# A last mixture-of-experts expert that norms its own rows, on one Trainium2 core

## The chip, the core and the metric

The kernel runs on one core of a Trainium2 chip. The metric is the device time of one execution in microseconds (us), over several runs. The engines are TensorE (PE, with its weight loads shown as PEld), VectorE (DVE), ScalarE (ACT), GpSimd (POOL) and SyncE (SP). DMAs are issued by SP, ACT and POOL; an issue takes its place in its engine's order, so an engine that waits before an issue does nothing else meanwhile.

## The reference

One post-norm layer over 512 tokens of 1024 features in float32: a layer norm, three mixers (differential attention, gated delta rule, S5), an output projection, a layer norm, and then a mixture of experts, whose sum is added to its own input and normed again:

```python
for e in range(16):
    hid = silu(h @ w1[e]) * (h @ w3[e])
    ffn += comb[:, e:e+1] * (hid @ w2[e])      # comb: 2 experts of 16 a token, else 0
out = layer_norm(ALPHA * h + ffn, ln2_g, ln2_b)
```

The change lies in the last two lines: when the sum of a token's row is complete, and when it is normed and stored. The kernel works on the row divided by ALPHA, which the norm's epsilon allows for.

## The kernel before, in words

Everything is in `tile_layer`. Up to some 495 us of the trace it computes the mixers, the first norm and the routing; the routing sorts the tokens into slots of each expert. `hdr` and `yd` (in DRAM) both hold the normed rows: `hdr` is what the experts read, `yd` is the running sum of row and experts.

**The experts.** Sixteen experts run one after the other. A "large" one has 128 slots and splits its weights into a high and a low part (`split`, ACT `e_hi` and DVE `e_lo`), a "small" one has 64 slots and uses them as loaded. Of the last three, 13 is large, 14 and 15 are small. `gather` (L1494) fetches an expert's token rows by an indirect DMA of POOL, and `turn_x` transposes them (ACT `xth`). Each expert has 12 weight chunks of 512 KB: 0 to 7 ("up": w1 and w3), after which ACT makes the Silu (`hid`) and DVE the product; `turn_h` transposes it (`hhh`); 8 to 11 ("down": w2) give its output in PSUM (`pS`). `finish` and `finish2` scale that by the token's weight (ACT, `y`, one buffer) and `scatter` (L1499) adds it to rows of `yd` by an indirect DMA of POOL that accumulates; a small expert's slots hold half rows, 64 on the first half of the partitions and 64 on the second.

**The order.** `steps` (L1606 to 1611) lists the 192 chunks: ups of expert e, then downs of e-1. The loads go out in that order on SP (`ahead`, L1632) into a ring of 34 buffers, whose places are given by `RING` (L42). The buffers are memory of the stage before, so the first load into each waits until that stage has done with it; load 28 also waits for the first two gathers (`FIRST`, L55). N is 192.

**The end.** Experts 0 to 13 are scattered, 14 and 15 are not: `y_parts` (L1697) splits their scaled output into a high and a low part, and one-hot matrices (built at step N-20 by POOL's iota and DVE) put their rows by matmuls onto PSUM banks (`add_y`, L1741), on top of the rows of `yd`, which SP loads as soon as scatter 13 has landed (L1734). The norm's parameters are loaded by SP after them (L1737). The four tiles of 128 rows are then normed from PSUM, spread over DVE, ACT and POOL (`sum_v`, `square_a`, `centre`, `rsqrt_a`, `last`), and SP stores them in seven pieces (`put`, L1845).

Of the kernel before, what the change touches and what calls it, by code (L numbers as in the profile page):

```python
# [21 lines left out]
P = 128  # L22
D = 1024
S = 512
# [17 lines left out]
RING = (2, 8, 15, 14, 21, 13, 12, 11, 9, 10, 29, 3, 7, 30, 18, 31, 16, 17, 19, 20, 27, 28, 6, 32, 33, 0, 1, 4, 5, 22, 23, 24, 25, 26)  # L42
OHT = 20
HT = 9
# [35 lines left out]
def tile_layer(ctx: ExitStack, tc: tile.TileContext, a, out):  # L80
# [157 lines left out]

    def place_init(e):
        e.memset(sb16[:, 0:64], 0.0)  # L240
        e.memset(half2[0:SL], 8192.0)
        e.memset(half2[SL:P], 8193.0)
        e.memset(fold2, 0.0)
        for h in range(2):
            e.tensor_copy(fold2[0:SL, h * SL:(h + 1) * SL], ident[0:SL, 0:SL])

# [1336 lines left out]
    def turn2(x, own=False):  # L1583
# [3 lines left out]
        h = halves(traw())[0] if own else exs("hhh", F32)  # L1587
        act(h[:, 0:4 * SL], p[:, 0:4 * SL], AF.Copy)
        return h
# [10 lines left out]
    def turn_h(e):  # L1600
        hts[e] = turn2(hid[e], e == NE - 1) if small[e] else turn(hid[e], "hh")
# [46 lines left out]
    def step(i):  # L1648
# [3 lines left out]
        if c < 8:  # L1652
# [11 lines left out]
            if c == 7:  # L1664
# [8 lines left out]
                if e == 0:  # L1673
                    turn_h(e)
        else:
# [6 lines left out]
            if e == NE - 2 and c == HT:  # L1682
                turn_h(e + 1)
            if c == 11:
                if e + 1 < NE - 1:
                    turn_h(e + 1)
                if e < NE - 2:
                    (finish2 if small[e] else finish)(pys[e][0] if small[e] else pys[e], at(1, e), at(0, e))
                else:
                    y_parts(e)  # L1690


    li = [ex.tile([P, 1], F32, name="li%d" % i) for i in range(2)]
    oht = []
    yps = {}

    def y_parts(e):  # L1697

        comb, p = at(1, e), pys[e][0]
        yh, yl = yps[e] = halves(traw(F32R))  # L1700
        act(yh, p, AF.Copy, scale=comb)
        stt(yl, p, comb, f32(yh), ALU.mult, ALU.subtract)
        tt(xgs[e % 2][:, 0:512], f32(yh), f32(yl), ALU.add, e=gp)

    with tc.manual_schedule():
# [7 lines left out]
        for i in range(N - 4):  # L1713
# [4 lines left out]
            if i == N - OHT:  # L1718
                io = traw()[:, 0:S]
                gp.iota(io, pattern=[[1, S]], base=-4096, channel_multiplier=0, allow_small_or_imprecise_dtypes=True)  # L1720
                oht.extend(halves(traw(F32R)))
                for j in range(2):

                    nc.vector.tensor_copy(li[j], at(0, NE - 2 + j))
                    ts(li[j], li[j], half2, ALU.subtract, 0.5, ALU.mult)
                    ts(oht[j], io, li[j], ALU.is_equal)
                nc.vector.tensor_copy(cnti, most)


    with tc.manual_schedule():  # L1730
        xs = {}
        for t in TORD:
            xs[t] = traw()
            nc.sync.dma_start(xs[t], yd[t * P:(t + 1) * P, :])  # L1734
        g2 = [traw(), traw()]
        for x, y in zip(g2, ("ln2_g", "ln2_b")):
            nc.sync.dma_start(x, a[y].partition_broadcast(P))  # L1737
        junk = [traw() for _ in range(2)]
        zs = {}

        def add_y(t, e):  # L1741

            for i, y in enumerate(yps[e]):
                for n in range(2):
                    r = slice(n * SL, (n + 1) * SL)
                    mm(zs[t][n], oht[e - NE + 2][r, t * P:(t + 1) * P], y[r], e < NE - 1 and i == 0, e == NE - 1 and i == 1)

        def pre(t):
            zs[t] = [psT(), psT()] if t == 3 else psS() if t == 1 else psA((NE - 1 + t // 2) % 2)
            add_y(t, NE - 2)  # L1750

        def add_h(t):

            for n in range(2):
                mm(zs[t][n], ident, xs[t][:, n * 512:n * 512 + 512], False, False)

        for i in range(N - 4, N):
            ahead(i + 1, CASTS2)
            step(i)
        act(junk[0][:, 0:1], pcol, AF.Copy)  # L1760
        table()

        for t in TORD[0:3]:
            pre(t)
        add_y(TORD[0], NE - 1)
        add_y(TORD[1], NE - 1)
        add_h(TORD[2])
        add_y(TORD[2], NE - 1)
        pre(TORD[3])
        add_h(TORD[3])  # L1770
        add_y(TORD[3], NE - 1)

        def exv(name, n):
            return ex.tile([P, n], F32, name=name)


        var, rr = {}, {}

        def pair(x):
            v, r = exv("var%d" % x, 2), exv("rr%d" % x, 2)  # L1780
            for j, t in enumerate((x, x + 1)):
                var[t], rr[t] = v[:, j:j + 1], r[:, j:j + 1]
            return v, r

        P0, P1 = pair(0), pair(2)

        def rsqrt_a(v, x):

            w, y, q = exv("w%d" % x, 2), exv("y%d" % x, 2), exv("q%d" % x, 2)
            ts(w, v, 1.0, ALU.mult, EPS2, ALU.add)  # L1790
            act(y, w, AF.Ln)
            act(y, y, AF.Exp, scale=-0.5)

            def end(r):
                tt(q, y, y, ALU.mult)
                tt(q, q, w, ALU.mult)
                ts(q, q, -0.5, ALU.mult, 1.5, ALU.add)
                tt(r, q, y, ALU.mult)

            return end  # L1800

        EPS2 = LN_EPS / ALPHA ** 2
        st = {t: ex.tile([P, 2, 6], F32, name="st%d" % t) for t in (2,)}
        mv = {t: exv("mv%d" % t, 2) for t in (2,)}
        hs, hq, nm = ({t: exv("%s%d" % (n, t), 2) for t in (0, 1, 3)} for n in ("hs", "hq", "nm"))

        def half(c):
            return slice(c * 512, c * 512 + 512)

        def bn(t, c):  # L1810
            nc.vector.bn_stats(st[t][:, c, :], zs[t][c])  # L1811

        def bn_end(t):
            nc.vector.bn_aggr(mv[t], st[t].rearrange("p a b -> p (a b)"))  # L1814
            nc.vector.tensor_copy(var[t], mv[t][:, 1:2])  # L1815

        def sum_v(t):

            for c in range(2):
                x = xs[t][:, half(c)]  # L1820
                nc.vector.scalar_tensor_tensor(x, zs[t][c], 1.0, x, ALU.mult, ALU.add, accum_out=hs[t][:, c:c + 1])
            zs[t] = halves(xs[t])

        def sum_a(t):
            for c in range(2):
                act(junk[0][:, half(c)], zs[t][c], AF.Identity, accum_out=hs[t][:, c:c + 1])

        def sum_end(t):

            ts(nm[t][:, 0:1], hs[t][:, 0:1], hs[t][:, 1:2], ALU.add, -1.0 / (32 * D), ALU.mult)  # L1830
            ts(nm[t][:, 1:2], hs[t][:, 0:1], hs[t][:, 1:2], ALU.add, -1.0 / D, ALU.mult)

        def square_a(t):

            for c in range(2):
                act(junk[0][:, half(c)], zs[t][c], AF.Square, scale=1.0 / 32, bias=nm[t][:, 0:1],
                    accum_out=hq[t][:, c:c + 1])

        def square_end(t):
            tt(var[t], hq[t][:, 0:1], hq[t][:, 1:2], ALU.add)  # L1840

        def centre(t, m, op, c):
            stt(xs[t][:, half(c)], zs[t][c], m, g2[0][:, half(c)], op, ALU.mult)

        def put(t, c):  # L1845
            nc.sync.dma_start(out[0, t * P:(t + 1) * P, c], xs[t][:, c])

        def last(t):
            for c in range(2):
                x = xs[t][:, half(c)]  # L1850
                stt(x, x, rr[t], g2[1][:, half(c)], ALU.mult, ALU.add)
                put(t, half(c))

        sum_v(1)
        sum_end(1)
        square_a(1)
        sum_v(0)
        xs[0] = junk[1]
        sum_end(0)
        square_a(0)  # L1860
        for c in range(2):
            centre(0, nm[0][:, 1:2], ALU.add, c)
        square_end(1)
        square_end(0)
        end = rsqrt_a(P0[0], 0)
        sum_a(3)
        end(P0[1])
        nb = exv("nb", 1)
        tt(nb, nm[1][:, 1:2], rr[1], ALU.mult)
        for c in range(2):  # L1870
            act(xs[1][:, half(c)], zs[1][c], AF.Identity, scale=rr[1], bias=nb)
        last(0)
        sum_end(3)
        for c in range(2):
            centre(3, nm[3][:, 1:2], ALU.add, c)
        square_a(3)
        for x, op in ((0, ALU.mult), (1, ALU.add)):
            for c in range(2):
                x_ = xs[1][:, half(c)]
                tt(x_, x_, g2[x][:, half(c)], op, e=gp)  # L1880
# [130 lines left out]
```

## Time and profile before

| | us |
|---|---|
| median of 3 runs | 772.11 (771.17 to 775.31) |
| the profiled execution | 778.69 |
| its span in the trace | 777.0 |
| PE busy / DVE / ACT / POOL, of the span | 685.4 / 523.8 / 352.9 / 101.6 |

The profiled execution is 1.7 us longer than its span, and 6.6 us over the median; all times in the rows are from the start of the span. Busy shares are means over stages with different limits. The experts' stage is 495 to 762 us, and what the change touches is from there to the end.

### The profile page before, as it was taken

How to read it: one execution, taken by the hardware profiler on the slowest of the kernel's cores; microseconds unless marked ns; L12 is line 12 of the kernel's file. 1: busy time of each engine (PE TensorE's matmuls, PEld its weight loads, DVE VectorE, ACT ScalarE, POOL GpSimd, SP SyncE). 2: the span in 40 equal slices, each digit the busy share in tenths (PEclk: the TensorE clock that was granted, in tenths of full speed). 3: DMA queues.
4: the chain of work that ended last, by engine and by line, in shares of the span. 5: the costliest groups of instructions: out<-in, count | busy, mean ns of one | idle time of the engine just before them, and what ended most of it. 6: DMA issues, size and time to landing. Idle time of an engine off the chain costs nothing. (4 is left out here: it accounts for less than half of the span.)

```text
span 777.0 us, 10787 instructions
## 1 busy us (share of the span) xinstructions
PE 685.4 (88%) x3560; PEld 499.1 (64%) x3560; DVE 523.8 (67%) x1375; ACT 352.9 (45%) x572; POOL 101.6 (13%) x138
## 2 busy tenths in 40 slices
PE   0999949999899799999899975789999999999881
PEld 0667737786788576667687754668655767677420
DVE  6899997786753445566737888879454577677326
ACT  2579632723111522155523321568464577566323
POOL 6010000000000011111000012111131132112112
PEclk9999978997778999959779995699999999999996
DMA  6142304120101257517314239899999999999983
GB/s 218 47 141 73 118 1 124 34 65 28 55 1 51 73 154 184 177 37 198 131 42 178 94 134 417 324 411 326 351 394 385 386 383 356 393 349 387 385 312 114
DMA packets 54271, 155.98 MB, mean 201 GB/s; under 512 B 13528, under 2 KB 13784, under 8 KB 54208
## 3 DMA queue, kind: packets, MB, share of 16 engines
q1 hardware_dynamic: 38960, 124.26, 42.1%
q0 software_dynamic: 8192, 19.08, 9.3%
q10 hardware_dynamic: 7056, 11.88, 5.1%
q8 instruction: 30, 0.49, 0.2%
q14 instruction: 33, 0.27, 0.1%
HBM read 139.98 MB, written 19.14 MB: 205 GB/s over the span
## 5 line engine op out<-in xcount | busy, mean ns | idle before, releaser
L84 DVE TENSOR_TENSOR e_lo<-e_raw,e_hi 128x1024 fp32r<-128x1024 f32 x108 | 128.7, 1222 | 28.3 <-ACT e_hi L95 24.6
L95 ACT ACTIVATE e_hi<-e_raw 128x1024 fp32r<-128x1024 f32 x108 | 111.7, 1061 | 29.0 <-PE pA L101 9.1
L101 PE MATMUL pA<-hTh,w_lo 128*128 128x512 f32 x184 | 76.8, 419 | 12.3 <-DVE w_lo L84 12.3
L101 PE MATMUL pA<-hTh,w_hi 128*128 128x512 f32 x184 | 78.3, 426 | 2.5 <-DVE cv L92 1.1
L101 PE MATMUL pA<-hTl,w_hi 128*128 128x512 f32 x184 | 75.5, 411 | 0.0
L101 PE MATMUL pA<-e_hi,xth 128*128 128x512 f32 x144 | 58.2, 404 | 0.0
L101 PE MATMUL pA<-e_lo,xth 128*128 128x512 f32 x144 | 57.1, 397 | 0.1
L101 PE MATMUL pA<-e_hi,xtl 128*128 128x512 f32 x144 | 57.2, 397 | 0.0
L101 PE MATMUL pA<-e_raw,xth 128*64 128x512 f32 x224 | 50.4, 596 | 0.0
L101 PEld LDWEIGHTS pA<-hTh,w_lo 128*128 128x128 f32 x184 | 36.3, 197 | 20.5 <-DVE w_lo L84 12.9
L95 ACT ACTIVATE w_hi<-w_raw 128x1024 fp32r<-128x1024 f32 x29 | 30.6, 1054 | 34.9 <-PE pA L101 26.0
L1500 POOL DMA_INDIRECT yd__140<-y,tab x14 | 23.2, 1658 | 172.0 <-ACT y L95 159.1
L101 PEld LDWEIGHTS pA<-hTh,w_hi 128*128 128x128 f32 x184 | 36.3, 197 | 12.6 <-issue 2.3
L101 PEld LDWEIGHTS pA<-hTl,w_hi 128*128 128x128 f32 x184 | 36.2, 197 | 7.6 <-issue 0.7
L84 DVE TENSOR_TENSOR w_lo<-w_raw,w_hi 128x1024 fp32r<-128x1024 f32 x29 | 35.2, 1218 | 2.6 <-ACT w_hi L95 2.4
L84 DVE TENSOR_TENSOR hid<-pA,hid 128x512 f32<-128x512 f32 (+1 forms) x16 | 11.0, 690 | 36.5 <-ACT hid L95 22.8
L101 PEld LDWEIGHTS pA<-e_raw,xth 128*64 128x64 f32 x224 | 15.8, 137 | 29.4 <-issue 27.3
L1495 POOL DMA_INDIRECT xg<-hdr,tab x16 | 30.3, 1896 | 28.5 <-PE pS L101 9.0
L1206 DVE TENSOR_REDUCE nm<-pA 128x1 f32<-128x128 f32 (+3 forms) x48 | 22.9, 484 | 13.8 <-PE pA L101 9.0
L101 PEld LDWEIGHTS pA<-e_lo,xth 128*128 128x128 f32 x144 | 27.6, 192 | 6.4 <-DVE e_lo L84 0.5
L101 PEld LDWEIGHTS pA<-e_hi,xth 128*128 128x128 f32 x144 | 27.6, 191 | 6.1 <-ACT xth L95 0.3
L101 PEld LDWEIGHTS pA<-e_hi,xtl 128*128 128x128 f32 x144 | 27.6, 192 | 6.0 <-DVE xtl L84 0.4
(522 smaller groups left out, 1484.2 us busy)
## 6 DMA issues: line engine op xcount, KB each, us to landing
e_raw<-in_moe_w_dram SPq DMA_DIRECT2D x192, 512.0 KB
w_raw<-in_w_cm_dram SPq DMA_DIRECT2D x12, 512.0 KB
w_raw<-in_w_cm_dram ACTq DMA_DIRECT2D x11, 512.0 KB
qks<-qkd POOLq DMA_DIRECT2D x18, 256.0 KB, 4.0
qkd<-qk SPq DMA_DIRECT2D x6, 512.0 KB
h0d<-x SPq DMA_DIRECT2D x4, 512.0 KB
w_raw<-in_w_out_dram SPq DMA_DIRECT2D x4, 512.0 KB
w_raw<-in_w_out_dram ACTq DMA_DIRECT2D x4, 512.0 KB
```

What stands on the lines that cost most here:

```text
L84: return e.tensor_tensor(o, x, y, op=op)
L95: return nc.scalar.activation(o, x, f, **kw)
L101: return nc.tensor.matmul(o, l, r, start=start, stop=stop)
L1206: nc.vector.tensor_reduce(nm[:, c:c + 1], pc[c][:, 0:nk], axis=AX.X, op=ALU.max, negate=True)
L1495: return nc.gpsimd.indirect_dma_start(out=xg, out_offset=None, in_=rows_of(hdr, n), in_offset=bass.IndirectOffsetOnAxis(ap=idx, axis=0), b ...
L1500: nc.gpsimd.indirect_dma_start(out=rows_of(yd, n), out_offset=bass.IndirectOffsetOnAxis(ap=idx, axis=0), in_=y, in_offset=None, bounds_che ...
```

## The change

Expert 14 is scattered like the others. All rows of `yd` are then loaded (by POOL, `xs`), normed and stored without expert 15's part. Expert 15's own 64 tokens (as 128 half rows, `own`) are gathered from `yd` too; its output is added to them in its slots, they are normed there (the two halves' statistics are joined by a matmul with `fold3`), and an indirect store writes them over their rows of `out`. Beside that the parameters are loaded by ACT, earlier; the last expert's ups come after the downs of 14; two ring buffers (3 and 6) move to the ring's end. The one-hot matrices and the adding matmuls go. The conditional block behind it (more tokens than slots) scatters expert 15 alone. The diff, cut:

```diff
-RING = (2, 8, 15, 14, 21, 13, 12, 11, 9, 10, 29, 3, 7, 30, 18, 31, 16, 17, 19, 20, 27, 28, 6, 32, 33, 0, 1, 4, 5, 22, 23, 24, 25, 26)
+RING = (2, 8, 15, 14, 21, 13, 12, 11, 9, 10, 29, 7, 30, 18, 31, 16, 17, 19, 20, 27, 28, 32, 33, 0, 1, 4, 5, 22, 23, 24, 25, 26, 3, 6)
...
-        steps += [(e, c) for c in (range(8) if small[e] else ORD)]
-        if e:
-            steps += [(e - 1, c) for c in range(8, 12)]
+        x = [(e, c) for c in (range(8) if small[e] else ORD)]
+        y = [(e - 1, c) for c in range(8, 12)] if e else []
+        steps += y + x if e == NE - 1 else x + y
...
             if i == N - OHT:
...
+                g2, gh = [traw(), traw()], halves(traw())
+                for x, h, y in zip(g2, gh, ("ln2_g", "ln2_b")):
+                    nc.scalar.dma_start(x, a[y].partition_broadcast(P))
+                    for n in range(2):
+                        nc.scalar.dma_start(h[n * SL:(n + 1) * SL], a[y][n * 512:n * 512 + 512].partition_broadcast(SL))
...
+        for t in TORD:
+            gp.dma_start(xs[t], yd[t * P:(t + 1) * P, :])
+        idx = at(0, NE - 1)
+        nc.gpsimd.indirect_dma_start(out=own[0], out_offset=None, in_=rows_of(yd, 2),
...
+        def stats():
+            for t in TORD:
+                c = slice(t, t + 1)
+                if t % 2:
+                    act(junk, xs[t], AF.Identity, accum_out=sums[:, c])
+                    ts(nm[t], sums[:, c], -1.0 / (32 * D), ALU.mult)
+                    ts(mean[:, c], sums[:, c], 1.0 / D, ALU.mult)
+                    act(junk, xs[t], AF.Square, scale=1.0 / 32, bias=nm[t], accum_out=var[:, c])
+                else:
+                    for n in range(2):
+                        nc.vector.bn_stats(st[t][:, n, :], xs[t][:, n * 512:n * 512 + 512])
...
+            rsqrt_c(rr, var, 0, NT)
+        def put(t):
+            x, c = xs[t], slice(t, t + 1)
+            stt(x, x, mean[:, c], g2[0], ALU.subtract, ALU.mult)
+            stt(x, x, rr[:, c], g2[1], ALU.mult, ALU.add)
+            nc.sync.dma_start(out[0, t * P:(t + 1) * P, :], x)
+        for i in range(N - 12, N):
             ahead(i + 1, CASTS2)
+            if i == N - 8:
+                stats()
+                put(TORD[0])
+                put(TORD[1])
             step(i)
+            if i == N - 5:
+                put(TORD[2])
+                put(TORD[3])
+                act(junk[:, 0:1], pcol, AF.Copy)
+                table()
...
+        stt(z, py, at(1, e), z, ALU.mult, ALU.add)
...
+        nc.vector.bn_stats(lst, z)
+        nc.vector.bn_aggr(lmv, lst)
+        mm(pm[:, 0:2], fold3, lmv)
...
+        rsqrt_c(lr, lv[:, 1:2], 1, 1)
+        stt(z, z, lv[:, 0:1], gh[0], ALU.subtract, ALU.mult)
+        stt(z, z, lr, gh[1], ALU.mult, ALU.add)
+        nc.gpsimd.indirect_dma_start(out=rows_of(out[0], 2), out_offset=bass.IndirectOffsetOnAxis(ap=idx, axis=0),
```

Here `rsqrt_c` is the former `rsqrt_a` in one piece, with Ln and Exp on ACT; `rr` holds all four tiles. Where a `step` is the last up chunk of expert 15 (N-5), the Silu, the product and `turn_h` are in it.

How this stands in the engines' orders is shown at three places. First ACT, from the transpose copy of expert 15's tokens (`xth`) on; `hhh` and the two `y` behind it are experts 14 and 13. Before:

```order
L95 ACTIVATE xth<-pT 128x512
L95 ACTIVATE hhh<-pT 128x256
L95 ACTIVATE y<-pS,tab_136 128x512 x2
L95 ACTIVATE hid<-pA 64x512
L95 ACTIVATE e_raw<-pT 128x256
```

and in the change, with each row's waits (DMAHW is the completion of loads of SP and ACT, counted in lanes that both use in turn; DMASW of POOL's; the number behind is the counter's):

```order
L1710 DMA e_raw<-in_ln_g_dram 128x1024 [waits DMAHW0_49]
L1712 DMA e_raw<-in_ln_g_dram 64x512 x2
L1710 DMA e_raw<-in_ln_b_dram 128x1024 [waits DMAHW5_49]
L1712 DMA e_raw<-in_ln_b_dram 64x512 [waits DMAHW7_49]
L1712 DMA e_raw<-in_ln_b_dram 64x512 [waits DMAHW0_49]
L94 ACTIVATE hhh<-pT 128x256 [waits DVE_49,PE_49]
L94 ACTIVATE y<-pS,tab_136 128x512 [waits DMASW2_49,Activation_49]
L94 ACTIVATE y<-pS,tab_136 128x512
L94 ACTIVATE y<-pS,tab_136 128x512 [waits DMASW3_49,PE_49,Activation_49]
```

The six parameter loads have come between `xth` and `hhh`, and a third `y`, that of expert 14, stands behind the two halves of expert 13's. The first and the last load name the same lane.

Second ACT again, right behind those rows, where the change norms the rows (`e_raw` are rows of `yd`, `hid` is expert 15's Silu):

```order
L94 ACTIVATE e_raw,sums<-e_raw 128x1024
L94 ACTIVATE e_raw,var<-e_raw,nm_6857 128x1024
L94 ACTIVATE e_raw,sums<-e_raw 128x1024
L94 ACTIVATE e_raw,var<-e_raw,nm_6858 128x1024
L94 ACT_TABLE_LOAD
L94 ACTIVATE y_6888<-w_6887 128x4
L94 ACT_TABLE_LOAD
L94 ACTIVATE y_6888<-y_6888 128x4
L94 ACT_TABLE_LOAD
L94 ACTIVATE hid<-pA 64x512
L94 ACTIVATE hhh<-pT 128x256
```

and DVE, from the rows' factor `rr` to expert 15's output:

```order
L83 TENSOR_TENSOR rr<-q_6889,y_6888 128x4
L91 SCALAR_TENSOR_TENSOR e_raw<-e_raw,mean 128x1024
L91 SCALAR_TENSOR_TENSOR e_raw<-e_raw,rr 128x1024
L91 SCALAR_TENSOR_TENSOR e_raw<-e_raw,mean 128x1024
L91 SCALAR_TENSOR_TENSOR e_raw<-e_raw,rr 128x1024
L83 TENSOR_TENSOR hid<-pA,hid 64x512
```

Before, `hid` of expert 15 followed on both engines what belongs to expert 14; now the statistics of all rows and the first two tiles' outputs are ahead of it. Behind `hid` DVE has the other two tiles, four more rows alike.

Third POOL's end. Before, its last rows of this kind are

```order
L1500 DMA yd__140<-y,tab_135 512x1024
L1720 IOTA e_raw 128x512
L1500 DMA yd__140<-y,tab_135 512x1024
L84 TENSOR_TENSOR xg_4573<-e_raw 128x512
```

and in the change

```order
L1504 DMA yd__140<-y,tab_135 512x1024 x2
L1504 DMA yd__140<-y,tab_135 1024x512
L1736 DMA e_raw<-yd__140 128x1024 x4
L1738 DMA e_raw<-yd__140,tab_135 128x512
L1800 DMA out_dram<-e_raw,tab_135 1024x512
```

The second of those counted x2 is scatter 13; behind it now come scatter 14, the four loads of rows that SP issued before, the gather of expert 15's rows and the last store.

## Rows read from the trace of the kernel before

**Rows 1.** Windows: stretch, length, busy PE PEld DVE ACT POOL (count), PEclk, DMA share, GB/s

```profile
560.00:680.00 120.00, 120.00 (x571) 76.40 (x570) 72.34 (x71) 71.28 (x91) 29.00 (x16) 1.00 1.03 383
...
728.00:745.00 17.00, 13.67 (x60) 5.69 (x60) 5.43 (x11) 4.61 (x8) 1.59 (x1) 1.00 0.96 356
...
762.00:777.00 15.00, 0.00 (x0) 0.00 (x0) 8.99 (x21) 2.33 (x7) 5.01 (x4) 0.56 0.38 144
```

**Rows 2.** Waits of SP's queue, whole run: what it waited for, us, times, longest

```profile
SPq L1632 <- DMA e_raw<-in_moe_w_dram: 120.8, 121, 3.3
SPq L1632 <- PE pT L1098: 25.0, 2, 24.7
...
SPq L1734 <- DMA yd__140<-y,tab: 4.6, 1, 4.6
```

**Rows 3.** Timeline of the end: start, us, engine, line, operation [idle before <-releaser]

```profile
751.11 0.20 PEld L101 LDWEIGHTS pA<-e_raw 128*64 128x64 f32 x4 [1.04 <-DMA e_raw<-in_moe_w_dram]
768.58 2.74 DVE L92 SCALAR_TENSOR_TENSOR e_raw<-e_raw,rr 128x512 f32<-128x512 f32 x4
761.59 10.09 SPq L1846 DMA_DIRECT2D out_dram<-e_raw  x7
```

**Rows 4.** Ahead of the experts: a window, POOL's first gathers, PE's first transposes

```profile
435.00:460.00 25.00, 21.64 (x140) 18.43 (x139) 21.06 (x68) 8.86 (x24) 1.08 (x2) 1.00 0.17 63
488.19 1.10 POOL L1495 DMA_INDIRECT xg<-hdr,tab  x1 [6.70 <-DVE aux L1423]
493.84 1.97 PE L1529 MATMUL pT<-ident,xg 128*128 128x128 f32 x8 [0.42 <-DMA xg<-hdr,tab]
```

**Rows 5.** Timeline of ACT, 728 to 735 us, and one DMA issue of it early

```profile
728.63 1.06 ACT L95 ACTIVATE e_hi<-e_raw 128x1024 fp32r<-128x1024 f32 x1 [0.18 <-DMA e_raw<-in_moe_w_dram]
730.08 0.58 ACT L95 ACTIVATE xth<-pT 128x512 f32<-128x512 f32 x1
732.75 0.39 ACT L95 ACTIVATE hhh<-pT 128x256 f32<-128x256 f32 x1 [2.09 <-PE pT L1586]
733.03 1.26 ACT L95 ACTIVATE y<-pS,tab 128x512 f32<-128x512 f32 x2
38.29 0.33 ACTq L704 DMA_DIRECT2D gb<-in_ln_in_g_dram  x1
```

**Rows 6.** Timeline: scatter 13 on POOL, and SP's loads of the rows behind it

```profile
734.57 1.59 POOL L1500 DMA_INDIRECT yd__140<-y,tab  x1 [13.95 <-ACT y L95]
743.69 2.77 SPq L1734 DMA_DIRECT2D e_raw<-yd__140  x4
```

**Rows 7.** DMA issues of POOL: operation, count, KB each, median us to landing

```profile
qks<-qkd POOLq DMA_DIRECT2D x18, 256.0 KB, 4.0
hdr<-xo POOLq DMA_DIRECT2D x4, 512.0 KB, 7.0
xg<-hdr,tab POOLq DMA_INDIRECT x16, 8.4
yd__140<-y,tab POOLq DMA_INDIRECT x14, 8.9
```

**Rows 8.** Timeline of ACT: a table load, the Silu behind it, a sum's read-out

```profile
504.41 1.28 ACT L95 ACT_TABLE_LOAD   x1
505.70 0.60 ACT L95 ACTIVATE hid<-pA 128x512 f32<-128x512 f32 x1
756.58 0.19 ACT L95 ACTIVATION_READ_ACCUMULATOR e_raw<-e_raw,nm 128x1 f32 x1
```

**Rows 9.** DVE: one group by form (busy, mean ns), then two timeline rows

```profile
L92 DVE SCALAR_TENSOR_TENSOR xo<-xo,ln_mv,g 128x1024 f32<-128x1024 f32 x4 | 5.1, 1280 | 0.7 <-PE pG L1331 0.7
741.17 0.69 DVE L84 TENSOR_TENSOR hid<-pA,hid 64x512 f32<-64x512 f32 x1 [7.70 <-ACT hid L95]
767.07 0.17 DVE L89 TENSOR_SCALAR w<-var 128x2 f32<-128x2 f32 x1
```

**Rows 10.** Timeline of PE: two chunks' down matmuls of a small expert

```profile
743.67 1.08 PE L101 MATMUL pS<-e_raw,hhh 128*64 128x512 f32 x4 [2.30 <-DMA e_raw<-in_moe_w_dram]
```

More of the change, by code (lines that the diff above doesn't have):

```diff
@@ L237, in tile_layer @@
     fold2 = stri
+    fold3 = triu
     def place_init(e):
@@ L245, in place_init @@
             e.tensor_copy(fold2[0:SL, h * SL:(h + 1) * SL], ident[0:SL, 0:SL])
+            for q in range(2):
+                r = slice(q * SL, (q + 1) * SL)
+                e.tensor_copy(fold3[r, h * SL:(h + 1) * SL], ident[r, r])
     def slot_all(oh, p):
@@ L1581, in up2, with turn2 @@
                 mm(p[h * SL:(h + 1) * SL], x[:, s_], w[h][:, j * 512:(j + 1) * 512], k == 0, k == KT - 1)
-    def turn2(x, own=False):
+    def turn2(x):
         p = psT()
@@ L1586, in turn2 @@
             nc.tensor.transpose(p[:, j * SL:(j + 1) * SL], x[0:SL, j * P:(j + 1) * P], ident[0:SL, 0:SL])
-        h = halves(traw())[0] if own else exs("hhh", F32)
+        h = exs("hhh", F32)
         act(h[:, 0:4 * SL], p[:, 0:4 * SL], AF.Copy)
@@ L1600, in turn_h @@
     def turn_h(e):
-        hts[e] = turn2(hid[e], e == NE - 1) if small[e] else turn(hid[e], "hh")
+        hts[e] = turn2(hid[e]) if small[e] else turn(hid[e], "hh")
     def gather_for(e):
@@ L1686, in step @@
                     turn_h(e + 1)
-                if e < NE - 2:
+                if e < NE - 1:
                     (finish2 if small[e] else finish)(pys[e][0] if small[e] else pys[e], at(1, e), at(0, e))
[L1689 to L1703, printed above, removed]
     with tc.manual_schedule():
@@ L1712, in tile_layer @@
         place_a(SA, scratch)
-        for i in range(N - 4):
+        for i in range(N - 12):
             ahead(i + 1, CASTS if i < N - SW else CASTS2)
@@ new lines, in tile_layer, with exv, rsqrt_c @@
+                g2, gh = [traw(), traw()], halves(traw())
[3 more added lines that the diff above has]
+                        nc.scalar.dma_start(h[n * SL:(n + 1) * SL], a[y][n * 512:n * 512 + 512].partition_broadcast(SL))
+    def exv(name, n):
+        return ex.tile([P, n], F32, name=name)
+    EPS2 = LN_EPS / ALPHA ** 2
+    def rsqrt_c(r, v, x, n):
+        w, y, q = exv("w%d" % x, n), exv("y%d" % x, n), exv("q%d" % x, n)
+        ts(w, v, 1.0, ALU.mult, EPS2, ALU.add)
+        act(y, w, AF.Ln)
+        act(y, y, AF.Exp, scale=-0.5)
+        tt(q, y, y, ALU.mult)
+        tt(q, q, w, ALU.mult)
+        ts(q, q, -0.5, ALU.mult, 1.5, ALU.add)
+        tt(r, q, y, ALU.mult)
@@ L1730, in tile_layer @@
     with tc.manual_schedule():
-        xs = {}
+        xs = {t: traw() for t in TORD}
+        junk, own = traw(), halves(traw())
         for t in TORD:
[L1733 to L1757, printed above, removed]
+            gp.dma_start(xs[t], yd[t * P:(t + 1) * P, :])
+        idx = at(0, NE - 1)
+        nc.gpsimd.indirect_dma_start(out=own[0], out_offset=None, in_=rows_of(yd, 2),
+                                     in_offset=bass.IndirectOffsetOnAxis(ap=idx, axis=0),
+                                     bounds_check=2 * S - 1, oob_is_err=False)
@@ new lines, in tile_layer @@
+        mean, var, rr, sums = (exv(x, NT) for x in ("mean", "var", "rr", "sums"))
+        st = {t: ex.tile([P, 2, 6], F32, name="st%d" % t) for t in (0, 2)}
+        mv = {t: exv("mv%d" % t, 2) for t in (0, 2)}
+        nm = {t: exv("nm%d" % t, 1) for t in (1, 3)}
+        def stats():
[9 more added lines that the diff above has]
+                        nc.vector.bn_stats(st[t][:, n, :], xs[t][:, n * 512:n * 512 + 512])
+                    nc.vector.bn_aggr(mv[t], st[t].rearrange("p a b -> p (a b)"))
+                    nc.vector.tensor_copy(mean[:, c], mv[t][:, 0:1])
+                    nc.vector.tensor_copy(var[:, c], mv[t][:, 1:2])
+            rsqrt_c(rr, var, 0, NT)
@@ L1761, in tile_layer @@
[L1761 to L1880, printed above, removed]
@@ L1881, in tile_layer @@
-        put(1, slice(0, D))
-        for c in range(2):
-            bn(2, c)
-        bn_end(2)
-        centre(2, mv[2][:, 0:1], ALU.subtract, 0)
-        square_end(3)
-        end = rsqrt_a(P1[0], 2)
-        centre(2, mv[2][:, 0:1], ALU.subtract, 1)
-        end(P1[1])
-        last(3)
-        last(2)
+            if i == N - 5:
[3 more added lines that the diff above has]
+                table()
+        e = NE - 1
+        py, z = pys[e][0], own[0]
@@ new lines, in tile_layer @@
+        stt(z, py, at(1, e), z, ALU.mult, ALU.add)
+        act(xgs[e % 2][:, 0:512], py, AF.Copy, scale=at(1, e))
+        lst, lmv, lv, lr = ex.tile([P, 6], F32, name="lst"), exv("lmv", 2), exv("lv", 2), exv("lr", 1)
+        nc.vector.bn_stats(lst, z)
+        nc.vector.bn_aggr(lmv, lst)
+        pm = psT()
+        mm(pm[:, 0:2], fold3, lmv)
+        ts(lv, pm[:, 0:2], 0.5, ALU.mult)
+        tt(lmv[:, 0:1], lmv[:, 0:1], lv[:, 0:1], ALU.subtract)
+        stt(lv[:, 1:2], lmv[:, 0:1], lmv[:, 0:1], lv[:, 1:2], ALU.mult, ALU.add)
```

17 lines of the change are left out of this document (3 added, 14 removed).

## The prediction

> **What bounds the kernel now.** I read the windows first, then SP's waits, then the timeline of the end.
>
> While the experts run, the DMA engines are busy all the time and move 383 GB/s, which is one chunk of 512 KB in 1.37 us; PE is busy too, at the granted clock 1.00 [rows 1]. But SP, which issues the weight loads, waits 121 times for a load of its own to complete, 120.8 us in all [rows 2]: the stream of weights sets the pace from some 495 to 751 us. Near its end it still moves 356 GB/s, with PE at 13.67 us of 17 [rows 1]. The last chunk is there at 751.11 [rows 3]. Behind it lies a tail of 777.0 - 751.1 = 25.9 us that is a chain of DVE, ACT and small matmuls: PE does nothing from 762 on and the DMA share is 0.38 [rows 1]. Its last pieces are four DVE operations from 768.58 and a store: SP's seven stores end their issue at 761.59 + 10.09 = 771.7, and the span ends 5.3 us later [rows 3]. So the change has two ways to gain: an earlier stream, or a shorter tail.
>
> Something that the tail needs was early before: scatter 13 is issued at 734.57 and has landed at 743.69, when SP's loads of the rows can go [rows 6]. That is 9.1 us, 7.4 us ahead of the last chunk.
>
> **The change, part by part**, on the times of the profiled execution.
>
> *Ring.* Buffer 3's first load waits 24.7 us for a PE operation of the stage before (from 435 to 460 us), and blocks all loads behind it on SP [rows 2]; in that window the DMA share is 0.17 [rows 4]. With it at the ring's end some 11 loads go earlier. But load 28 waits for the first gathers, issued at 488.19, and PE, which starts the experts at 493.84, waited only 0.42 us for them [rows 4]. I take -0.4 us, this wait; the bounds are 0 and -1.7, if the gathers' 5.65 us from issue to use fell to the 4.0 of another 256 KB transfer [rows 7] and the routing ahead of them on PE shrank as much.
>
> *ACT is held.* `xth` ends at 730.66 [rows 5], now 730.3. Then ACT issues six loads, 1.5 MB, at 0.33 us each [rows 5]; the last waits for the lane of the first, that is for the first load's landing. A 512 KB load under traffic took 7.0 us, 256 KB took 4.0 [rows 7]; I take 7.0, with 4.0 to 8.9 as ends (8.9 is the longest median of the table). So the last issue is done at 730.3 + 7.0 + 0.3 = 737.6. `hhh` (0.39) and `y` of expert 13 (1.26) [rows 5] follow: 739.3. Scatter 13 is issued at 739.5 in place of 734.57, and with its 9.1 us [rows 6] it lands at 748.6.
>
> *Two scatters in a row.* `y` has one buffer, so expert 14's `y` (0.7, as [rows 9] for half the size on DVE) waits for that landing: 749.3; scatter 14 is issued at 749.5. What it takes lies between the first gathers' 5.65 us [rows 4] and 9.1 [rows 6]; the stream ends meanwhile (751.1 - 0.4 + 4.1 for 1.5 MB more at 383 GB/s = 754.8), so I take 7.5: 757.0. The downs of 14 now stand behind an up chunk of 15 on PE; that costs nothing, since `y` waits longer.
>
> *Loads of the rows.* They are issued at 757.0, behind the scatter on POOL's queue, on nearly quiet DMA engines. The nearest row is 4.0 us for 256 KB [rows 7]; then each next 512 KB needs 1.37 us: 761.0, 762.4, 763.7, 765.1. By the Trainium skill, "DMA: Bandwidth & Descriptors", section "Anatomy of one DMA — SWDGE (gpsimd) path", such a DMA takes about 2.0 us and its bytes at 436 GB/s, an estimate of 3.2 us here; the kernel's median of 4.0 us for half the bytes speaks against it, and by it the sum would be 0.8 lower.
>
> *Statistics on ACT*, for tiles 1 and 3: a pass over 1024 columns is 1.06 us [rows 5], its read-out 0.19 [rows 8]; DVE's small operation between two passes about 0.35 (twice 0.17 [rows 9]). The second tile's two passes start with the third tile's landing at 763.7, or when the first two end (761.0 + 2.9 = 763.9): with 2.9 us each, 766.8. DVE's two tiles (each under 2 us) are beside this, the last landing at 765.1: 766.9 as well.
>
> *Three table loads*, for Ln, Exp and back to Silu: 1.28 us each [rows 8], with two small activations of 0.2 and the Silu's 0.60: 766.8 + 3.84 + 0.4 + 0.6 = 771.7. In the trace the Silu starts at once behind its load [rows 8]. The Trainium skill, "ScalarE: Activation LUTs", section "What ACT_TABLE_LOAD costs", has a drain of some 1.38 us beside the load; by it the sum would be 4.1 higher, and the row shows none behind the load.
>
> *DVE between.* `rr` needs four small operations after Exp (769.8): 770.6. Then, ahead of expert 15's product, four operations of 128x1024 at 1.28 [rows 9]: 775.7. The product, 0.69 [rows 9], ends at 776.4. This is the step that I hold for the costliest: the last expert's hidden product, ready to be made at some 750 by its weights, waits for the norm of all other rows. Four more such operations end at 781.5. PE's transpose, `hhh` and the downs (0.46, 0.39, and eight matmuls, twice 1.08 [rows 5, 10], 3.0 in all, or 5.6 if PE's part doubles, since PE's granted clock was 0.56 where it idled [rows 1], near the lower of its two levels, 1.2 GHz of 2.4) end at 779.4 to 782.0, beside the DVE work.
>
> *The own rows.* z, bn, and two last operations, each 0.69 [rows 3] for 512 columns: 2.8; small ones and the matmul 1.2; `rsqrt_c` 1.5 (its tables are loaded already): 781.5 + 5.5 = 787.0.
>
> *The store.* Before, the end came 5.3 us after the last store's issue [rows 3]. The indirect one needs POOL 1.59 [rows 6] in place of 0.33: 6.6, and it waits for the four plain stores, of which the last (issued 781.5, landed 786.8) is in time. 793.6.
>
> What goes: the one-hot matmuls, y_parts and the norm from PSUM, all in the former tail, whose 25.9 us are replaced by this chain. **Sum**: 793.6 - 777.0 = +16.6 us. Made against the profiled execution this is 778.69 + 16.6; against the median of the runs, 6.6 lower, it is 772.1 + 16.6 = **788.7 us**.
>
> **Rivals.**
>
> *A, the other side: the norm of the rows hides under the stream.* From the issue of the row loads to expert 15's product I count 776.4 - 757.0 = 19.4 us, from there to the end 17.2. If the loads were issued at 740.4 or earlier, the end would be no later than before, and at 733.6, where the stream's own end takes over, it would come 6.8 us earlier: 765.3 us. For it: the DMA engines and DVE have room under 751. Against: scatter 13 alone landed at 743.7 before [rows 6] and scatter 14 comes behind it. 0.03.
>
> *B: ACT isn't held* (the lane's load is there at once, or the lane is another). Scatter 13 goes as before at 734.2, `y` of 14 at 743.3, scatter 14 at 744.2 lands under the full stream at 753.3. The loads of rows then share with the stream until 754.8, so that the chain is some 2.5 us earlier: +14, 786.2 us. It is the same chain with its first wait shorter. 0.25.
>
> *C: dear ends.* Scatter 14 at 9.1, the first row load at 7.0 [rows 7] in place of 4.0, and PE at the lower clock 0.5: +5, 793.7 us. A drain at the table loads would lead there too. 0.18.
>
> *D: the change doesn't tell* in the time, within 0.5% (3.9 us, what a measurement of this kernel can tell from no change): two or three mis-sized terms of one sign (an own chain beside the rows' stores, scatters of 4 us each) would be needed to lose 13 us. 0.02.
>
> **How the numbers follow.** Forecast 0.52, B 0.25, C 0.18, A 0.03, D 0.02. The range: below, the bounds of B with quick DMAs (scatter 14 at 5.65 in place of 9.1, and the ring's -1.7) reach 786.2 - 5.2 = 781; above, C with a little more, 796. It leaves out A, D and the rest of C, less than 2 in 10. Faster by over 0.5%: A, 0.03; within: 0.02; slower: 0.95.
>
> **What would show it right or wrong.** Right: ACT idle some 6 us behind `xth` with its own load as releaser; scatter 13 issued about 739.5; two landings, near 749 and 757; row loads from 757; three table loads near 767 to 771; the product of expert 15 near 776 with PE idle before it for over 10 us; a last store on POOL near 787 and nothing behind it. PE should show no work between the stream's end and that product. The weights end near 755, not 751. Wrong: if row loads are issued under 741, or the product comes ahead of the rows' operations, or the end is ruled by the plain stores. If the experts start over 2 us earlier, the ring was worth more than I took.

## The result, and the profile after

The changed kernel takes 795.22 us (median of 4 runs, 793.48 to 800.73), the kernel before 773.71 in the same measurement: the ratio is 1.0274 (1.0225 to 1.0323), that is 17 to 25 us slower; the ratio leaves out a slow run of the kernel before (787.54 us). Forecast were 788.7 us and +16.6, with a range of 781 to 796. The sign, the mechanism and the range held, the range by less than 1 us; the size was some 5 us short.

The profiled execution took 800.73 us with a span of 799.0, 22.0 more than the span before; as before, it is one of the longer ones (5.5 over its median, before 6.6), so the spans' difference and the medians' (21.5) agree.

The windows of the changed kernel (columns as in [rows 1]):

```profile
435.00:460.00 25.00, 21.35 (x139) 18.18 (x138) 21.11 (x68) 8.82 (x25) 1.08 (x2) 0.99 0.74 268
560.00:680.00 120.00, 120.00 (x574) 76.19 (x572) 74.72 (x73) 73.35 (x93) 29.00 (x16) 1.00 1.02 382
762.00:777.00 15.00, 2.09 (x8) 1.03 (x10) 10.82 (x20) 9.00 (x13) 0.00 (x0) 0.50 0.20 81
777.00:799.00 22.00, 5.03 (x16) 1.39 (x12) 6.75 (x15) 1.09 (x3) 1.05 (x1) 0.58 0.15 58
```

The experts' stretch is as it was (382 GB/s for 383, PE busy throughout [rows 1]). The loads that stood behind buffer 3 now go early: 268 GB/s from 435 to 460 in place of 63 [rows 4]. All the loss is behind the experts.

ACT's timeline there, answering to [rows 5, 8]:

```profile
726.14 0.34 ACTq L1710 DMA_DIRECT2D e_raw<-in_ln_g_dram  x1
...
727.44 0.58 ACT L94 ACTIVATE xth<-pT 128x512 f32<-128x512 f32 x1
...
729.68 4.22 ACTq L1712 DMA_DIRECT2D e_raw<-in_ln_b_dram  x2
734.00 0.38 ACT L94 ACTIVATE hhh<-pT 128x256 f32<-128x256 f32 x1 [5.98 <-DMA e_raw<-in_ln_b_dram]
...
745.51 0.69 ACT L94 ACTIVATE y<-pS,tab 128x512 f32<-128x512 f32 x1 [9.97 <-DMA yd__140<-y,tab]
758.25 1.06 ACT L94 ACTIVATE e_raw<-e_raw 128x1024 f32<-128x1024 f32 x1 [12.05 <-DMA e_raw<-yd__140]
...
764.92 1.28 ACT L94 ACT_TABLE_LOAD   x1
766.21 0.20 ACT L94 ACTIVATE y<-w 128x4 f32<-128x4 f32 x1
766.44 1.28 ACT L94 ACT_TABLE_LOAD   x1
...
769.25 0.59 ACT L94 ACTIVATE hid<-pA 64x512 f32<-64x512 f32 x1
```

Three waits stand one behind the other: 5.98 us for its own parameter loads, 9.97 for scatter 13, 12.05 for the rows. The first parameter load is issued at 726.14, 1.3 us before `xth` starts, though `xth` stands ahead of it in ACT's order: here an issue did not wait for the operations ahead of it to be executed, while `hhh`, behind the last issue, did wait for that issue. Expert 15's Silu is at 769.25, where before its product was made at 741.17 [rows 9]. POOL's timeline, answering to [rows 6], shows what lies between:

```profile
735.82 1.57 POOL L1504 DMA_INDIRECT yd__140<-y,tab  x1 [18.54 <-ACT y L94]
746.47 1.55 POOL L1504 DMA_INDIRECT yd__140<-y,tab  x1 [9.08 <-ACT y L94]
754.65 2.26 POOL L1736 DMA_DIRECT2D e_raw<-yd__140  x4 [6.62 <-issue]
...
787.75 1.05 POOL L1800 DMA_INDIRECT out_dram<-e_raw,tab  x1 [29.46 <-DVE e_raw L91]
```

The row loads go at 754.65, in place of 743.69 [rows 6]. The view names no releaser for them ("issue"); that they waited for scatter 14 is shown below, by leaving it out. DVE's timeline, from the rows' factor to the last expert's last operation:

```profile
768.57 0.16 DVE L83 TENSOR_TENSOR rr<-q,y 128x4 f32<-128x4 f32 x1
...
773.70 0.68 DVE L83 TENSOR_TENSOR hid<-pA,hid 64x512 f32<-64x512 f32 x1
...
778.12 1.29 DVE L91 SCALAR_TENSOR_TENSOR e_raw<-e_raw,rr 128x1024 f32<-128x1024 f32 x1
781.73 0.75 DVE L91 SCALAR_TENSOR_TENSOR e_raw<-pA,tab,e_raw 128x512 f32<-128x512 f32 x1 [2.32 <-PE pA L100]
...
786.71 0.75 DVE L91 SCALAR_TENSOR_TENSOR e_raw<-e_raw,lr 128x512 f32<-128x512 f32 x1
```

and PE's, on both sides of the product:

```profile
749.81 1.93 PE L100 MATMUL pA<-e_raw,xth 128*64 128x512 f32 x6 [0.17 <-DMA e_raw<-in_moe_w_dram]
774.43 0.68 PE L1590 MATMUL pT<-ident,hid 64*128 64x64 f32 x4 [22.69 <-DVE hid L83]
775.59 6.09 PE L100 MATMUL pA<-e_raw,hhh 128*64 128x512 f32 x16 [0.47 <-ACT hhh L94]
```

PE has its last up matmuls at 749.81 and then waits 22.69 us for the product. The chain of work that ended last goes through just these pieces (a few of its 81, start and length):

```profile
746.47 1.55 DMA yd__140<-y,tab
748.03 6.60 issue
...
755.84 6.37 DMA e_raw<-yd__140
...
775.59 6.12 PE pA L100 x16
```

**The forecast's steps against the trace** (us from the span's start):

| step | forecast | seen |
|---|---|---|
| ACT's last parameter issue done | 737.6 | 733.9 |
| scatter 13 issued | 739.5 | 735.8 |
| scatter 14 issued | 749.5 | 746.5 |
| row loads issued | 757.0 | 754.65 |
| rows' factor `rr` made | 770.6 | 768.7 |
| product of expert 15 made | 776.4 | 774.4 |
| first own operation starts | 781.5 | 781.7 |
| last own operation done | 787.0 | 787.5 |
| end of the span | 793.6 | 799.0 |

### The profile page after: what moved, and what is told of

It reads as the page before. It is cut to its first block, busy times and chain, and to the rows that moved or that the text cites. A ratio compares the mean times of both kernels' runs of the same rounds, so it can differ in the third digit from the quotient of the medians.

```text
span 799.0 us, 10696 instructions
## 1 busy us (share of the span) xinstructions
PE 681.5 (85%) x3522; PEld 496.6 (62%) x3522; DVE 523.8 (66%) x1363; ACT 354.4 (44%) x565; POOL 100.6 (13%) x142
## 5 line engine op out<-in xcount | busy, mean ns | idle before, releaser
L100 PE MATMUL pA<-e_raw,xth 128*64 128x512 f32 x224 | 54.3, 601 | 6.1 <-DMA e_raw<-in_moe_w_dram 6.1
L1504 POOL DMA_INDIRECT yd__140<-y,tab x15 | 24.7, 1646 | 183.8 <-ACT y L94 183.8
```

The source lines that it names most:

```text
L100: return nc.tensor.matmul(o, l, r, start=start, stop=stop)
L1504: nc.gpsimd.indirect_dma_start(out=rows_of(yd, n), out_offset=bass.IndirectOffsetOnAxis(ap=idx, axis=0), in_=y, in_offset=None, bounds_che ...
```

## The experiments

The stretch ahead of the experts differs from execution to execution whatever the kernel: the Silu of expert 13 starts between 695.0 and 709.0 us in these traces. So, beside the times, one span is read within each trace: **from the start of expert 13's Silu to the end of the span**. Before it is 777.0 - 705.65 = 71.3 us (the texts below say 71.2, read to the last event), in the changed kernel 799.0 - 703.00 = 96.0. What the change costs is so 24.7 us there; the rest, 2.6 us in these two traces, was gained ahead of it. The runs that leave the tail as it is tell how well this reading repeats: 71.5, 71.5 and 72.0 for three with the tail of before, 95.8 for one with the changed tail. So a difference of 3 us in it can be read from one trace each.

### The ring

One line in the kernel before:

```diff
-RING = (2, 8, 15, 14, 21, 13, 12, 11, 9, 10, 29, 3, 7, ..., 28, 6, 32, ..., 26)
+RING = (2, 8, 15, 14, 21, 13, 12, 11, 9, 10, 29, 7, ..., 28, 32, ..., 26, 3, 6)
```

> The kernel before with the new ring alone (buffers 3 and 6 at the ring's end). Theory of the profiles: the loads that stood behind buffer 3 are in memory before the first gathers, so these land sooner (PE's first transposes 0.9 us earlier), and PE keeps its higher clock after its 3.4 us wait at 510 us, where it fell for some 3.5 us before (another 1.7 us). Everything behind is then 2.6 us earlier: -2.6 us against before, some 0.34% faster. Rival, the term that was predicted: -0.4 us, as PE waited only 0.4 us for the gather. Rival: 0, the stream of weights sets the pace anyway.

Measured: ratio 0.999 (0.9947 to 1.0033), 772.88 us for 773.75, 71.5 us from expert 13's Silu. A gain as small as that can't be told from none here. Its counterpart, the same line undone in the changed kernel:

> The changed kernel with the former ring. If the ring is worth 2.6 us, it is that much slower than the changed kernel: +24 us against before in place of +21.5. If it is worth 0.4, +22. In the trace the Silu of expert 1 is again at 522.0 in place of 519.4.

Measured: 800.98 us, ratio 1.0363 (1.0289 to 1.0437), and 95.8 us from expert 13's Silu. The tail is the changed kernel's to 0.2 us, so the ring has no part in the loss. Ahead of the experts the first gather was issued at 481.39 and the Silu of expert 1 at 515.37:

```profile
481.39 1.10 POOL L1499 DMA_INDIRECT xg<-hdr,tab  x1 [6.69 <-DVE aux L1427]
...
515.37 0.58 ACT L94 ACTIVATE hid<-pA 128x512 f32<-128x512 f32 x1
```

34.0 us, much as before (33.8). In the twelve traces with the new ring it is 31.5 us in seven and 33.1 to 33.7 in five. Windows of 5 us from 513.4, first of the kernel before, then of the changed one (the third figure from the end is the granted clock):

```profile
513.40:518.40 5.00, 5.00 (x17) 4.06 (x18) 2.46 (x3) 1.86 (x3) 0.00 (x0) 0.66 1.03 420
```

```profile
513.40:518.40 5.00, 5.00 (x23) 4.12 (x23) 3.38 (x4) 3.57 (x4) 0.00 (x0) 1.00 1.03 419
```

Behind its wait of 3.21 us near 510, which both kernels have, PE fell to a clock of 0.66 in the one and not in the other, which is 1.6 us from the Silu of expert 0 to that of expert 1. Of the 2.6 us between the two traces, 0.9 was there before that wait. The twelve traces part by this clock too: 0.66 in the five slower ones, 1.00 in the seven others. In the changed kernel with the former ring, the 34.0 us come about in another way; its windows are

```profile
488.00:494.00 6.00, 6.00 (x17) 4.04 (x16) 4.68 (x9) 4.98 (x6) 1.05 (x1) 0.50 0.76 245
...
509.00:514.00 5.00, 5.00 (x25) 4.13 (x24) 3.16 (x4) 3.68 (x4) 0.00 (x0) 1.00 1.03 418
```

The clock stayed high behind the same wait, but ahead of it was still at 0.50 until 496.4, 15 us behind the gather's issue, where before it was at 1.00 from 10 us on. What goes with the ring in every trace is smaller: PE's first transposes start 5.65 and 5.73 us behind the first gather's issue with the former ring (488.19 to 493.84 before [rows 4]), and 5.05 to 5.08 us in all twelve with the new one; in the changed kernel's:

```profile
487.88 1.10 POOL L1499 DMA_INDIRECT xg<-hdr,tab  x1 [6.70 <-DVE aux L1427]
...
492.95 1.95 PE L1533 MATMUL pT<-ident,xg 128*128 128x128 f32 x8
```

That is 0.6 us for the ring; the rest of the 2.6 differs from execution to execution. The same edit was measured again, for its time alone:

> The kernel before with the new ring, once more, for its time alone. In the traces so far the stretch from the first gather's issue to the Silu of expert 1 is 33.8 and 34.0 us with the former ring, 31.5 us in half of those with the new one and 33.1 to 33.6 in the others, where PE's granted clock is down for a while behind its wait near 510 us. Theory: the ring gives 0.4 to 2.5 us, some 1.3 on average, 0.2%, which this measurement can't tell from nothing. Rival: it gives 2.6 always, 0.34%, and the two measurements together show it.

Measured: ratio 0.9978 (0.995 to 1.0006), 773.75 us for 775.06. Both intervals hold 1, both medians lie below. A gain of 0.1 to 0.2% would fit and is not shown.

Since the DMA engines are quiet ahead of the gathers with the new ring, one more constant was moved on top of it (`FIRST = 28` to `FIRST = 32`):

> The kernel before with the new ring, and with load 32 in place of load 28 as the one that waits for the first gathers. With the new ring the DMA engines are quiet ahead of the gathers (24 GB/s to 130 GB/s in the stretch 480 to 488 us in three traces), and the buffers of loads 28 to 31 are free by some 478 us. Theory: four loads of 1.37 us go there, and the stream is 5.5 us further on; PE waited for weights or for parts made from them some 5 us from 500 to 752, near the end above all, so that the end comes 3 to 5 us earlier than before, 0.4 to 0.6%. Rivals: PE is the bound where the stream is not, and the lead is lost again at the ring's 34 buffers: no more than the ring alone, -1 to -2; or the loads delay the gathers, as in the kernel before: 0.

Measured: ratio 0.9996 (0.996 to 1.0031), 72.0 us from expert 13's Silu. The lead of four loads changed nothing that can be measured: the rival was right, and the theory, that PE's waits for weights would go, wrong. The lead was soon given back: from 505 to 530 us the stream moved 307 GB/s in that run and 398 with the new ring alone (both have the first gather at 480.93), which is 2.3 MB less, about the four loads. So it isn't shown that the stream alone sets the pace from 495 us on, as the prediction read it; in the same rows PE is busy 120.00 of 120.00 us [rows 1].

### The product's place

```diff
-            if i == N - 8:
-                stats()
-                put(TORD[0])
-                put(TORD[1])
             step(i)
             if i == N - 5:
+                stats()
+                put(TORD[0])
+                put(TORD[1])
                 put(TORD[2])
```

> The changed kernel with the last expert's last up step (Silu, product, transposes) ahead of the statistics and the first two tiles' outputs. Theory: the product (774.4 in the changed kernel's trace) goes to some 753, PE's transposes and downs after it too, and the end is then set by DVE: eight operations of 1.27 us from 768.65 on, so that the last expert's first own operation starts at 778.8 in place of 781.7: -2.9 us against the changed kernel, +18.6 against before. Rival: if the end hung on the product alone, -20 us; if the plain stores set it, 0.

Measured: 92.6 us from expert 13's Silu (792.8 - 700.22), 3.4 less; in time 795.95 us, ratio 1.0285 (1.0195 to 1.0376), too wide to show 3 us. DVE's timeline of that run:

```profile
749.16 0.69 DVE L83 TENSOR_TENSOR hid<-pA,hid 64x512 f32<-64x512 f32 x1 [22.85 <-ACT hid L94]
765.37 1.28 DVE L91 SCALAR_TENSOR_TENSOR e_raw<-e_raw,mean 128x1024 f32<-128x1024 f32 x1
...
774.23 1.28 DVE L91 SCALAR_TENSOR_TENSOR e_raw<-e_raw,rr 128x1024 f32<-128x1024 f32 x1
775.55 0.75 DVE L91 SCALAR_TENSOR_TENSOR e_raw<-pA,tab,e_raw 128x512 f32<-128x512 f32 x1
```

The product is 22 us ahead of where it was (48.9 us behind expert 13's Silu in place of 70.7), and the end only 3.4: behind it waits nothing that isn't also behind the rows' eight operations on DVE (765.37 to 775.5). The prediction called the product's place the costliest step; it isn't. It is worth 3.4 us, since the rows' norm is the longer of two branches.

### ACT's own loads

```diff
-                    nc.scalar.dma_start(x, a[y].partition_broadcast(P))
+                    nc.sync.dma_start(x, a[y].partition_broadcast(P))
```

and the same for the four half loads.

> The changed kernel with the six parameter loads on SP's queue behind the weights in place of ACT's. Theory: ACT no longer waits for its own load (5.98 us ahead of expert 14's transpose copy at 734.00), scatter 13 goes at 732.0 in place of 735.8, and as scatter 14, the row loads and all behind them hang on its landing, the end comes 3 to 3.8 us earlier: +18 against before. Rival: the loads of rows now share with the parameters, and the stream's end with the scatter: 0.

Measured: 92.8 us (799.3 - 706.51), 3.2 less; 793.93 us, ratio 1.024 (1.0163 to 1.0317). Scatter 13 stands 29.0 us behind expert 13's Silu in place of 32.8, which is where it was before the change (734.57 - 705.65 = 28.9):

```profile
735.47 1.57 POOL L1504 DMA_INDIRECT yd__140<-y,tab  x1 [15.12 <-ACT y L94]
...
754.10 2.26 POOL L1736 DMA_DIRECT2D e_raw<-yd__140  x4 [7.15 <-DMA e_raw<-in_ln_g_dram]
```

ACT was held by its own loads, as predicted; this fells rival B, in which it wasn't. The row loads go 4.1 us earlier, but their first use comes 5.3 us behind the issue in place of 3.6, so that 3.2 us are left at the end.

### The second scatter

```diff
-                if e < NE - 1:
+                if e < NE - 2:
                     (finish2 if small[e] else finish)(...)
```

> The changed kernel without expert 14's scaled output and its scatter (expert 14's part of the sum is left out). Theory: two accumulating scatters stand one behind the other, and the loads of the rows wait for both. Without the second the loads go when scatter 13 has landed, 745.5 in place of 754.65 in the changed kernel's trace: the end comes 9.1 us earlier, 87 us from the Silu of expert 13 to the end in place of 96.0. The loads then share with the end of the stream, which takes some 1 to 2 us of it back. Rival: the product's place on DVE or the parameters set the end: 96.

Measured: 90.4 us (785.4 - 695.00), 5.6 less, not 7 to 8. The row loads did go 8.9 us earlier, 42.7 us behind expert 13's Silu in place of 51.6. But they now run while the weights still do:

```profile
733.00:745.00 12.00, 9.34 (x34) 2.72 (x30) 0.00 (x0) 0.61 (x1) 3.32 (x5) 1.00 1.02 387
```

This is the window of their issue and landing in that run: 387 GB/s, the full stream. ACT's timeline of it has the first row 6.7 us behind the issue at 737.68, where it was 3.6 in the changed kernel:

```profile
744.39 1.06 ACT L94 ACTIVATE e_raw<-e_raw 128x1024 f32<-128x1024 f32 x1 [16.85 <-DMA e_raw<-yd__140]
```

So an earlier issue is worth less than its lead while weights still stream: 3.3 us of 8.9 were given back.

### The last store

```diff
-        nc.gpsimd.indirect_dma_start(out=rows_of(out[0], 2), ...)
+        nc.sync.dma_start(rows_of(out[0], 2)[0:P, :], z)
```

> The changed kernel with a plain store of SP for the last indirect one of POOL (so the last expert's rows go to the first 64 rows and not to their own places; nothing else is left out). In the changed kernel's trace the span ends 11.5 us after the last operation on these rows, of which the transfer is in the first 4. Theory: what is left is POOL's end of a transfer that it issued itself, which SP's stores don't have (before: 5.6 us from the last issue to the end). The end then comes 5.5 us earlier: 90.5 us from the Silu of expert 13 to the end of the span, in place of 96.0. Rival: any last store costs this, as it has to wait for the four others: 96.

Measured: 89.9 us (798.9 - 709.04), 6.1 less. The same plain store, issued by POOL (`nc.gpsimd.dma_start`):

> As the run with SP's plain store, but issued by POOL (the last expert's rows go to the first 64 rows). If POOL's queue is the cause, the end is as late as in the changed kernel: 96 us from the Silu of expert 13. If the indirect form is, it is 5 us earlier, 91.

Measured: 96.4 us (796.9 - 700.54), nothing gained. The issue of the last store, first in the run with SP, then in that with POOL:

```profile
793.36 0.33 SPq L1800 DMA_DIRECT2D out_dram<-e_raw  x1
```

```profile
784.76 0.59 POOL L1800 DMA_DIRECT2D out_dram<-e_raw  x1 [29.09 <-DVE e_raw L91]
```

From there to the end of the span it is 5.5 us with SP, 12.1 with POOL, and 11.3 with POOL's indirect store of the changed kernel. All the runs part in this way: 11.0 to 12.1 us in the seven traces of the changed tail where POOL issues the last store, 5.5 to 6.5 in the three where SP does. In the changed kernel's the windows show that the bytes have moved by 791, and then nothing:

```profile
789.00:791.00 2.00, 0.00 (x0) 0.00 (x0) 0.00 (x0) 0.00 (x0) 0.00 (x0) 0.50 0.24 82
791.00:793.00 2.00, 0.00 (x0) 0.00 (x0) 0.00 (x0) 0.00 (x0) 0.00 (x0) 0.50 0.00 0
793.00:799.00 6.00, 0.00 (x0) 0.00 (x0) 0.00 (x0) 0.00 (x0) 0.00 (x0) 0.50 0.00 0
```

The store has landed 3.2 us behind its issue, by the list of DMA issues of that trace. So it isn't the indirect form and not the wait for the other stores, but that POOL issued the program's last transfer. What POOL does in these 8 us the views don't show, and it stays open.

### Together

The product ahead of the norm, the parameters on SP, and one table load ahead of the statistics (the tables hold Ln and Exp both, and the Silu is done by then):

> The changed kernel with the parameters on SP's queue, the last expert's product ahead of the rows' norm, and one table load for Ln and Exp ahead of the statistics in place of three behind them. Measured from the Silu of expert 13 to the end of the span, the changed kernel has 96.0 us and the kernel before 71.2. Theory: the terms add up: parameters -3.2 and product -3.5 as they were measured alone, and two loads of 1.28 us that stood between the statistics and the rows' outputs -2.6: 86.7 us, +12 to +13 us against before with the new ring's gain. Rival: the loads of rows, now earlier, share with the stream and the parameters and give half of it back: 91.

Measured: 789.26 us for 774.62, ratio 1.0191 (1.0126 to 1.0256): +14.6 us, where the changed kernel has +21.5. Within the trace (of the longest of four executions, so read roughly) it is 89.6 us (797.0 - 707.39), 6.4 less, between the theory's 9.3 less and the rival's 5. The terms don't quite add up: the last expert's first own operation comes 7.2 us earlier there, and the last store takes 0.7 longer.

With the second scatter and POOL's store taken out as well:

> As the run with the three changes, and without expert 14's scaled output and scatter (its part of the sum is left out), and with SP's plain store at the end (the last expert's rows go to the first 64 rows). Theory: -5.7 and -6.1 more, as measured alone: 75 us from the Silu of expert 13 to the end, within 4 us of the kernel before; what is left over of the difference is then the norm of the rows and that of the last expert one behind the other. Rival: the row loads now start ahead of the stream's end, and the stream's end with all that is behind it takes the place of the chain: over 80.

Measured: 80.6 us (778.2 - 697.62). The theory's 75 was too low: the rows' loads run under the stream here too. What still differs from the kernel before, 9.2 us, was tested by leaving out half of the rows' outputs:

```diff
-            stt(x, x, mean[:, c], g2[0], ALU.subtract, ALU.mult)
-            stt(x, x, rr[:, c], g2[1], ALU.mult, ALU.add)
+            if t in TORD[0:2]:
+                stt(x, x, mean[:, c], g2[0], ALU.subtract, ALU.mult)
+                stt(x, x, rr[:, c], g2[1], ALU.mult, ALU.add)
```

> As the run with all five, and without the four output operations of two of the four row tiles (tiles 3 and 2 are stored as they are, not normed; the rest left out is as there). That run has 80.6 us from the Silu of expert 13 to the end, 9.2 more than the kernel before. Theory: its end hangs on DVE, where eight operations of 1.28 us on the rows stand ahead of the last expert's own: without four of them 5.1 us less, 75.5. Rival: the stores of the rows, or the end of the stream behind them, set the end: 80.6 still.

Measured: 74.5 us (776.1 - 701.63), 6.1 less, of which 5.3 lie ahead of the last expert's first own operation and 0.8 in the last store. DVE's timeline of that run:

```profile
763.11 1.28 DVE L91 SCALAR_TENSOR_TENSOR e_raw<-e_raw,rr 128x1024 f32<-128x1024 f32 x1
764.43 0.75 DVE L91 SCALAR_TENSOR_TENSOR e_raw<-pA,tab,e_raw 128x512 f32<-128x512 f32 x1
```

The last expert's operation starts at once behind the rows' fourth, so DVE sets that end, at 1.28 us for each of the operations ahead. Before, this work was spread over DVE, ACT and POOL, and the last experts' rows needed no chain of their own behind it.

No version with the change's tail was as fast as the kernel before, not even those that leave work out, and the ring alone, the only part that may help, isn't told from it.

## Why the prediction was right, and where its sizes were off

**The chain.** Parameter loads on ACT, scatter 13, scatter 14, row loads, statistics, tables, DVE, own rows, store: each step is in the trace in that order, and the intervals between them were off by 1 us or less from scatter 13's issue to the product. The two scatters took 9.7 and 8.2 us to the next step (forecast 9.1 and 7.5), the first row 3.6 (4.0). The step "ACT is held" is shown by its undoing (-3.2 us). From the end of `xth` to the last issue done it took 5.9 us, 1.4 less than forecast, since the first load was issued ahead of `xth` and not behind it. The 7.0 us taken for that load were right by luck: the row they come from, `hdr<-xo` [rows 7], is of stores into DRAM; from the first issue to the last one done it was 7.8, for a forecast of 7.3. What was short here and what was long in the scatters, the row loads and the statistics (1.8 us together) nearly cancel.

**The first row load.** 3.6 us from issue to use. The Trainium skill, "DMA: Bandwidth & Descriptors", section "Anatomy of one DMA — SWDGE (gpsimd) path", gave an estimate of 3.2, the row 4.0; the trace lies between, and neither would have moved the sum by more than 0.4.

**The drain at the table loads.** By rows, Ln starts at 766.21, as the load of 764.92 ends; none is behind it. The forecast took the rows' price, and the trace agrees. The 1.38 us that the Trainium skill, "ScalarE: Activation LUTs", section "What ACT_TABLE_LOAD costs", adds beside each load did not come, so its sum, 4.1 us higher, was not the one to take.

**Two sizes were off, and one term met a lucky execution.**

- *Store* was the term that failed most: 6.6 us were taken for the last store and the end, from SP's 5.3 and POOL's longer issue; it took 11.5 us from the last operation. The nearest row, another engine's store, did not carry the price: with SP's store it is 5.5 to 6.5, with POOL's 11 to 12. It alone is 5 of the 5.4 us by which the end of the span was missed.
- *PE in "DVE between"*: 3.0 to 5.6 us were held to lie beside the 5.1 of DVE. From product to first own operation it was 7.35. [rows 10] is one chunk's downs and not two's, as the heading of those rows has it, so that four chunks are 16 records and 4.3 us at full clock; and the granted clock was 0.50 in the window 762 to 777 and 0.58 in the next, so that they took 6.09 (the forecast priced eight of them, 2.2 us). PE took DVE's cover away and cost 2.3 us.
- *Ring*: -0.4 was taken, -2.6 stood between the two traces, outside the bounds of 0 to -1.7. But only 0.6 us of it, in the gathers, is there in every trace with the new ring. The rest was mostly the clock behind a wait, which differs from execution to execution; by the runs' times the ring's worth is too small to be shown.

The last two nearly cancel in this pair of traces, by luck, so what the forecast fell short by is the store.

**The costliest step** was misnamed. The product that waits for the norm looked the worst in the order, but moving it gave 3.4 us. Dearer are the second scatter (5.6 us) and POOL's store (6.1), and of the rest, the rows' eight operations that stand on DVE one behind the other (6.1 us for half of them, in the run with the five other costs taken out).

**Rivals.** A (the norm hides under the stream) needed the row loads at 740.4; they came at 754.65. B fell with the parameters on SP. The measured 795.22 us lie nearer to C's 793.7 than to 788.7, but not for C's reasons: the second scatter (8.2 us) and the first row (3.6) were cheaper than C had them, no drain came, only the low clock of PE did, and the store, which made the difference, was in no rival. D was out by five times the bound.

## What to carry to other kernels

A serial tail is priced by walking each queue from wait to wait; that an operation is ready early and placed late says little until the branch beside it has been walked too. A chain of accumulating scatters into the same rows costs its full latency for each link (9.7 and 8.2 us here), and loads that follow gain less than their lead as long as another stream fills the DMA engines. Issue the program's last transfer from SP where it can be had (6.1 us here), and compare kernels within the trace from a common event where the stretch ahead of it varies by more than the effect.

## What the hardware showed that was not expected

- A last transfer issued by POOL ends the span 11.0 to 12.1 us after its issue, plain or indirect, against 5.5 to 6.5 us for SP's, though the bytes have moved some 3 us after the issue.
- The same wait of 3.2 us on PE was followed by a granted clock of 0.66 over the next 5 us in the kernel before and 1.00 in the changed one, whose instructions there are the same; of the twelve traces with the new ring, five have 0.66 and seven 1.00.
- ACT issued a DMA 1.3 us before an operation started that stands ahead of it in ACT's order (issue at 726.14, `xth` at 727.44).
